# A two-column norm-weight tile is allocated behind the work buffers of the second sweep

## The chip, the core and the metric

The kernel runs on one core of a Trainium2 chip. A core has five engines that work side by side and wait for each other by semaphores: TensorE (PE, matrix products into PSUM), VectorE (DVE), ScalarE (ACT), GpSimd (POOL) and SyncE (SP, which here does nothing but issue DMA transfers, in its program's order). The metric is the device time of one execution in microseconds (us), the median of several runs. Changes under about 0.2% can't be told from none.

## The reference

One layer of an encoder over 2048 positions of width 1024, in float32. One input projection feeds two groups of heads. Group A is gated linear attention with a decay, summed over a forward and a backward scan in chunks. Group B is multi-head latent attention: low-rank q and kv with RMS norms, a shared rotary key, a full softmax. Both are gated, concatenated, projected once more, and added to the input under a layer norm:

```python
def hybrid_mixer(x, positions, w_in, ...):
    h = x @ w_in
    (g_q, g_k, g_v, g_gate, g_lr_f, g_lr_b, m_cq, m_ckv, m_kr, m_gate) = split(h)
    o_a = gla_branch(g_q, g_k, g_v, g_gate, g_lr_f, g_lr_b, ...)
    o_b = mla_branch(m_cq, m_ckv, m_kr, m_gate, positions, q_norm_g, w_uq, kv_norm_g, w_ukv)
    return concatenate([o_a, o_b]) @ w_out
x = layer_norm(alpha * x + hybrid_mixer(x, ...))
```

`mla_branch` normalises the compressed query with the weights `q_norm_g`, 256 numbers, before the product with `w_uq`. These 256 numbers are the tile that the change is about.

## The kernel before

Almost every product is made of three matmuls (`mm3`, lines 418 to 422): each float32 operand is split into a high part and a low remainder (`hi`, line 366, a copy on ACT; `lo`, line 372, a subtraction on DVE or POOL), and high times high (L420), one cross product (L421) and the other (L422) are summed in PSUM.

The work has four stages in time. The *first sweep* (`sweep_a`) goes backwards over 16 chunks of 128 positions and makes group A's projections, the scans' local parts and the gates; it stores its results (`qd_s`, `oi_s`, `su_s`, `u_s`) in DRAM. Two gates that are left over, of chunks 15 and 14, are made at its end (`late_gates`): the products `ipg` from the operands `xbh`, `xbl` (the split input of the chunk) and `wgh`, `wgl`, 24 matmuls for each chunk. The *second sweep* (`sweep_c`) goes forwards in eight steps of two chunks. It makes group B's projections (`ipm`, lines 1250 and on), gate (`pz`), the compressed keys, the query products `pqr` and `pq`, and finishes group A: `Ob` (L1418, L1419) is the product of the stored q (`qdb`, split to `qhb`, `qlb`) with the state. The state is carried by POOL: L1387 decays it, L1390 adds the stored `SU` of a chunk, L1395 scales it into `SU`, and `SU` is split to the two halves of `MMb` (L366 on ACT, L372 on POOL). Then comes *attention*, with `pS` and `o` as its large products, and at last the *output projection* with layer norm.

Before the first step the second sweep sets up weights (`SETUP_C`). `su_lset` (line 1131) issues seven loads on SP, in this order: `gq` (the q norm weights as 128 partitions of two numbers), `gkv_b`, `wkr` twice (`wqr` and `wkT` lie in the two halves of one tile of that name), `wqT`, and two small columns. `absorb_w` (L1165) then multiplies `wqT` with `wkT` on PE into `pabs`; `su_wS` (L1152, L1154) scales `gq` and then `wqr` by it on ACT; `scale_w` (L1170, DVE) scales `pabs` by `gq` and `gkv_b`. The loads of the first `SU` come behind these on SP.

The order of the instructions on each engine in the second sweep is set by a table of places (`PLACE_C` and the tables for the first and last step): every part has a number, the parts are sorted by it, and each engine works through its own in that order. The scheduler adds the waits. One of its rules matters here: a tile may be written only after the last use of whatever lay on the same bytes before (`reuse_waits="tile"`), so an address decides what a load waits for.

The on-chip memory is filled from two sides. On the left lie the constants, the input buffers, then for the second sweep the pools `wz`, `wm`, `bc` (weights and the split input `xch`, `xcl`), `wl` (loaded group A data: `ub`, `oib`, `qdb`, `SU`), `wk2` (work tiles; in the code `w1`) and `smc` (small tiles of norm sums; in the code `sm`). On the right lie, among others, the tiles of the late gates (`xab` with `xbh` and `xbl`, `wgp` with the gate weights). A pool's tile takes a multiple of 32 bytes in each partition.

Of the kernel before, what the change touches and what calls it, by code (L numbers as in the profile page):

```python
# [9 lines left out]
F32 = mybir.dt.float32  # L10
# [8 lines left out]
P = 128  # L19
# [336 lines left out]
class K:  # L356
# [773 lines left out]

    def su_lset(self):
        nc, ins, w1 = self.nc, self.ins, self.w1
        self.gq = self.bc.tile([P, 2], F32, name="gq")
        self.gkv_b = w1.tile([P, H, P], F32, tag="oT", name="gkv_b")[:, 0]
        t1 = w1.tile([P, 2, 512], F32, tag="qa", name="wkr")
        self.wkT = t1[:, 0].rearrange("p (h l) -> p h l", h=H)
        self.wqr = t1[:, 1].rearrange("p (c d) -> p c d", c=2)
        self.wqT = w1.tile([P, H, 256], F32, tag="gm", name="wqT")
        for t, n in ((self.gq, "gq_col"), (self.gkv_b, "gkv_bc"), (self.wqr, "wqr"), (self.wkT, "wkT"),
                     (self.wqT, "wqT"), (self.gkv_c, "gkv_col"), (self.gn_c, "gn_col")):  # L1140
            nc.sync.dma_start(t, ins[n])
        self.wa = [None, None]
# [869 lines left out]
```

## Time and profile before

| | |
|---|---|
| median of 3 runs | 1317.59 us |
| lowest and highest run | 1316.13 and 1318.52 us |
| profiled execution, first to last instruction (span) | 1311.9 us |
| mean granted clock of TensorE in it | 0.998 |
| PE busy | 1288.3 us, 98% of the span |
| DVE, ACT, POOL busy | 73%, 62%, 60% |
| first sweep and late gates | 0 to some 373 us of the span |
| second sweep | some 373 to 620 us |
| attention | some 620 to 1180 us |

The profiled execution is known by its span alone; the runs are timed from outside and include what lies around it. In the rows below, PE, DVE, ACT and POOL are the engines, SPq is the issuing of a DMA on SP's queue, L and a number is the line of the kernel. A row of the order of time has the start in us of the span, the duration in us, the engine, the line, the operation, the tile written and the tiles read, and in brackets the idle time of the engine just before it and who ended it. A row of a group has, after the bar, the busy time in us and the mean duration in ns. Matmuls are pipelined, so rows of PE overlap.

### The profile page before, as it was taken

What the parts mean: (1) busy time and instruction counts of PE and PEld (TensorE: products, weight loads), DVE (VectorE), ACT (ScalarE), POOL (GpSimd) and SP (SyncE); (2) the same over time, 40 slices, a digit from 0 to 9 for tenths busy, and PEclk for the clock granted to TensorE, in tenths of its full rate; (3) what the DMA queues carried; (4) which work ended last, traced back from release to release, by engine and by line L of the source; (5) the groups of instructions that cost most, each with busy time, mean ns of one, the idle gap of its engine ahead of it and who ended that gap; (6) DMA issues with size and microseconds to landing.
All of it is one profiled execution on the core that took longest, in us unless ns stands there. A gap on an engine that the chain in (4) does not pass through costs nothing.

```text
span 1311.9 us, 19981 instructions
## 1 busy us (share of the span) xinstructions
PE 1288.3 (98%) x7081; PEld 1129.9 (86%) x7081; DVE 958.5 (73%) x1712; ACT 812.5 (62%) x1339; POOL 784.6 (60%) x494
## 2 busy tenths in 40 slices
PE   7999999999999999999999999999999999999997
PEld 7999999999989999999788888888888887888786
DVE  7967684655675455554888888888888888468998
ACT  6765656555575656564687787888888888511110
POOL 0143333232457666671388888889999999844441
PEclk9999999999999999999999999999999999999999
DMA  8131313122475555565301111112223210366663
GB/s 283 61 100 53 93 53 92 49 76 71 147 245 173 197 194 177 201 202 177 121 1 41 41 42 41 41 57 59 63 66 102 51 41 9 121 208 174 210 195 121
DMA packets 107819, 145.81 MB, mean 111 GB/s; under 512 B 17250, under 2 KB 62694, under 8 KB 107720
## 3 DMA queue, kind: packets, MB, share of 16 engines
q1 hardware_dynamic: 99128, 142.41, 35.0%
q0 software_dynamic: 672, 2.10, 0.4%
q8 instruction: 56, 0.92, 0.3%
q10 hardware_dynamic: 7920, 0.03, 0.3%
q14 instruction: 43, 0.35, 0.2%
HBM read 94.14 MB, written 50.36 MB: 110 GB/s over the span
## 4 chain that ended last, share of the span: by engine, by line
PE 83%; DVE 4%; DMA 3%; ACT 2%; issue 2%; POOL 1%; SPq 1%; DVEq 0%; POOLq 0%; ACTq 0%
PE o L420 4%; PE o L421 4%; PE pS L1521 4%; PE pS L1524 4%; PE o L422 4%; PE pS L1523 4%; PE pS L1525 4%; PE pS L1522 4%; PE ipa L420 4%; PE ipa L422 4%; PE ipa L421 4%; PE pz L421 2%; PE pz L420 2%; PE pz L422 2%; PE ipg L420 2%; PE ipg L421 2%
## 5 line engine op out<-in xcount | busy, mean ns | idle before, releaser
L372 POOL TENSOR_TENSOR pl<-s,ph 128x1024 fp32r<-128x1024 f32 x128 | 306.9, 2412 | 66.7 <-ACT ph L366 61.5
L1543 DVE TENSOR_TENSOR rm<-pS,rm 128x512 f32<-128x512 f32 x210 | 144.8, 690 | 44.1 <-ACT s L1530 39.0
L1530 ACT ACTIVATE s<-pS 128x1024 f32<-128x1024 f32 x128 | 131.2, 1025 | 67.6 <-PE pS L1525 65.6
L1567 DVE TENSOR_TENSOR s<-s,mb 128x1024 f32<-128x1024 f32 x128 | 151.2, 1213 | 9.5 <-PE mb L1561 9.3
L1030 POOL TENSOR_TENSOR Us<-Us,cw 128x512 f32<-128x512 f32 x16 | 18.5, 1157 | 227.0 <-DVE Us L1028 175.2
L366 ACT ACTIVATE ph<-s 128x1024 fp32r<-128x1024 f32 x128 | 135.0, 1057 | 18.1 <-PE o L422 17.6
L1571 ACT ACTIVATE s<-s 128x1024 f32<-128x1024 f32 x128 | 131.4, 1050 | 13.8 <-DVE s L1567 13.7
L420 PE MATMUL ipa<-wah,xah 128*128 128x384 f32 (+1 forms) x384 | 130.6, 340 | 6.8 <-ACT wah L366 6.8
L422 PE MATMUL ipa<-wah,xal 128*128 128x384 f32 (+1 forms) x384 | 125.2, 326 | 0.0
L421 PE MATMUL ipa<-wal,xah 128*128 128x384 f32 (+1 forms) x384 | 125.0, 325 | 0.0
L1521 PE MATMUL pS<-qh,ckvT_h 128*128 128x512 f32 x256 | 103.7, 405 | 0.7 <-ACT s L1571 0.4
L420 PE MATMUL o<-ph,vh 128*128 128x512 f32 x256 | 102.6, 401 | 0.0
L422 PE MATMUL o<-ph,vl 128*128 128x512 f32 x256 | 101.3, 396 | 0.0
L1524 PE MATMUL pS<-rh,krs 128*128 128x512 f32 x256 | 101.2, 395 | 0.0
L421 PE MATMUL o<-pl,vh 128*128 128x512 f32 x256 | 101.1, 395 | 0.0
L1523 PE MATMUL pS<-qh,ckvT_l 128*128 128x512 f32 x256 | 100.9, 394 | 0.0
L1525 PE MATMUL pS<-rl,krs 128*128 128x512 f32 x256 | 100.7, 393 | 0.0
L1522 PE MATMUL pS<-ql,ckvT_h 128*128 128x512 f32 x256 | 100.6, 393 | 0.0
L1594 DVE TENSOR_TENSOR ap<-ap,s 128x512 f32<-128x512 f32 x120 | 83.1, 693 | 2.7 <-ACT s L1571 0.8
L372 POOL TENSOR_TENSOR ol<-of,oh 128x512 fp32r<-128x512 f32 x32 | 43.0, 1346 | 65.6 <-ACT oh L366 65.6
L420 PEld LDWEIGHTS ipa<-wah,xah 128*128 128x128 f32 x384 | 73.5, 192 | 7.6 <-ACT wah L366 6.8
L420 PE MATMUL pz<-xch,wzh 128*128 128x256 f32 x256 | 74.8, 292 | 0.0
(325 smaller groups left out, 3856.4 us busy)
## 6 DMA issues: line engine op xcount, KB each, us to landing
xcf<-xT_dram SPq DMA_DIRECT2D x16, 512.0 KB, 4.7
xr<-x_dram SPq DMA_DIRECT2D x16, 512.0 KB, 6.5
out_dram<-rr SPq DMA_DIRECT2D x32, 256.0 KB, 2.0
xaf<-xT_dram SPq DMA_DIRECT2D x14, 512.0 KB, 4.2
oib<-oi_s SPq DMA_DIRECT2D x16, 256.0 KB, 4.1
qdb<-qd_s SPq DMA_DIRECT2D x16, 256.0 KB, 4.6
SU<-su_s SPq DMA_DIRECT2D x16, 256.0 KB, 4.4
ub<-u_s SPq DMA_DIRECT2D x16, 256.0 KB, 4.7
```

Source lines behind the costliest of these rows:

```text
L366: return nc.scalar.activation(dst, src, AF.Copy).ins
L372: return e.tensor_tensor(dst, src, hi.bitcast(F32), ALU.subtract).ins
L420: mm(out, ah, bh, start=start, stop=False)
L421: mm(out, ah, bl, start=False, stop=False)
L422: mm(out, al, bh, start=False, stop=stop)
L1521: mm(ps[:, e], kh, qh, start=True, stop=False)
L1522: mm(ps[:, e], kh, ql, start=False, stop=False)
L1523: mm(ps[:, e], kl, qh, start=False, stop=False)
L1524: mm(ps[:, e], kr, rh, start=False, stop=False)
L1525: mm(ps[:, e], kr, rl, start=False, stop=True)
L1543: V.tensor_tensor(d["rm"], src[:, e], d["rm"], ALU.max)
L1567: V.tensor_tensor(s, s, d["mb"][:, None, :].to_broadcast([P, 2, QB]), ALU.subtract)
```

## The change

One line: the tile `gq` is taken from the pool `sm`, which is opened after the work buffers, in place of `bc`, which lies before them.

```diff
     def su_lset(self):
         nc, ins, w1 = self.nc, self.ins, self.w1
-        self.gq = self.bc.tile([P, 2], F32, name="gq")
+        self.gq = self.sm.tile([P, 2], F32, name="gq", bufs=1)
         self.gkv_b = w1.tile([P, H, P], F32, tag="oT", name="gkv_b")[:, 0]
```

In the built program this does the following. `gq` moves from byte 120000 of each partition to byte 178880. All tiles of `wl` and `wk2` move down by the 32 bytes that `gq` took in front of them, so their start addresses leave 192 modulo 256 where they left 224. The tiles of `sm`, and everything in attention, stay where they were. The instructions and their order on each engine are the same. Four waits differ: the load of `gq` waits for PE's count 2,255 (before 2,152), since its bytes now lie in `xbh` of chunk 14; the loads of `gkv_b` and `wqT` no longer wait for PE (before, counts 2,200 and 2,214); and the high split of the first output weight, `woh0`, on ACT waits for three DMA queues (before, four).

## The prediction

> **What bounds the kernel now.** I read the page first (shares, then the chain that ended last), then PE's waits in the second sweep, then, because the edit touches a load on SP's queue, the order of time of each engine around the start of that sweep.
>
> ```profile
> span 1311.9 us, 19981 instructions
> PE 1288.3 (98%) x7081; PEld 1129.9 (86%) x7081; DVE 958.5 (73%) x1712; ACT 812.5 (62%) x1339; POOL 784.6 (60%) x494
> PE 83%; DVE 4%; DMA 3%; ACT 2%; issue 2%; POOL 1%; SPq 1%; DVEq 0%; POOLq 0%; ACTq 0%
> ```
>
> TensorE is busy 98% of the span and holds 83% of the chain. So whatever stops PE is paid in full, and whatever any other engine does is free until it makes PE wait. PE's own waits from 375 to 460 us of the span (who was waited for, total, times, longest) are these:
>
> ```profile
> PE Ob L1419 <- POOL qlb L372: 0.8, 1, 0.8
> PE ipm L422 <- POOL xcl L372: 0.4, 1, 0.4
> PE Ob L1418 <- DVE gm L1209: 0.3, 1, 0.3
> ```
>
> There is next to nothing to win there, and the first row shows a place without slack: at the first Ob product of the sweep, PE already waits for POOL.
>
> **The change part by part.** No instruction is added, removed or reordered on any queue. Three things change: addresses of the work buffers, the place of the 8-byte tile gq, and the waits that follow from what lay at these places before.
>
> *The wait of gq's load.* The old place was last used by tiles of the first sweep; the new one lies inside xbh of chunk 14, the stationary operand of the last late gate. In the built program the load is therefore released at PE's 2,255th count in place of the 2,152nd: the last read of that xbh, the L421 matmul below. SP's queue as it stood:
>
> ```profile
> 365.26 0.38 SPq L1141 DMA_DIRECT2D gq<-gq_col_dram  x1
> 365.74 0.38 SPq L1141 DMA_DIRECT2D gkv_b<-gkv_bc_dram  x1
> 369.60 0.33 SPq L1141 DMA_DIRECT2D wkr<-wqr_dram  x1
> ...
> 370.50 1.22 SPq L1141 DMA_DIRECT2D wqT<-wqT_dram  x1
> ...
> 372.98 0.84 SPq L1369 DMA_DIRECT2D SU<-su_s  x2
> ```
>
> ```profile
> 372.89 0.39 PE L421 MATMUL ipg<-wgl,xbh 128*128 128x512 f32 x1
> ...
> 378.00 0.37 PE L422 MATMUL ipm<-wmh,xcl 128*128 128x448 f32 x1
> 378.21 1.95 PE L1165 MATMUL pabs<-wkr,wqT 128*128 128x128 f32 x16
> ```
>
> That matmul ends at 372.89 + 0.39 = 373.28, so gq is issued at 373.3 in place of 365.26. Everything behind it on SP waits too. The queue itself lost some of this time before, so not all 8 us count: gkv_b came 0.48 after gq, and then wkr stood until 369.60 for a store of the first sweep:
>
> ```profile
> SPq L1141 <- DMA su_s<-Us: 3.3, 1, 3.3
> ```
>
> By 373 that store is long down. So wkr goes out at 373.28 + 0.48 + 0.48 = 374.24, which is 4.6 later than 369.60, and the loads behind it keep their spacing: wqT at 375.1, SU at 377.6. The PE waits that gkv_b and wqT lose had been met before their issue, and cost nothing either way.
>
> Who waits for these loads? Two things on PE's path. First pabs, which reads wkr and wqT:
>
> ```profile
> wqT<-wqT_dram SPq DMA_DIRECT2D x1, 512.0 KB, 4.9
> ```
>
> It landed at 370.50 + 4.9 = 375.4, with 2.8 us of cover before pabs at 378.21. Landing at 380.0 it breaks that cover by 1.8 us. Second, POOL's chain that makes the operands of the first Ob product. It begins with SU:
>
> ```profile
> 378.48 1.66 POOL L1390 TENSOR_TENSOR Sf<-Sf,SU 64x512 f32<-64x512 f32 x1 [5.37 <-DMA SU<-su_s]
> 380.21 1.37 POOL L1395 TENSOR_TENSOR SU<-Sf,cw 64x512 f32<-64x512 f32 x1
> 381.66 1.03 POOL L1387 TENSOR_TENSOR Sf<-Sf,cw 64x512 f32<-64x512 f32 x1
> ...
> 384.30 1.29 POOL L372 TENSOR_TENSOR MMb<-SU,MMb 128x512 fp32r<-128x512 f32 x1
> 385.56 1.27 POOL L372 TENSOR_TENSOR qlb<-qdb,qhb 128x512 fp32r<-128x512 f32 x1
> ```
>
> ```profile
> 385.75 0.28 PE L1418 MATMUL Ob<-MMb,qhb 128*128 128x256 f32 x1
> 386.88 0.33 PE L1419 MATMUL Ob<-MMb,qlb 128*128 128x128 f32 x1 [0.85 <-POOL qlb L372]
> ```
>
> POOL sits idle 5.37 us until SU lands, then runs without a break to 386.83, and PE waits for that. If SU lands 4.6 later, POOL starts at 383.1. It then runs a little faster: the first two of its operations ran beside DVE's eight wzl splits, which will be over by then, and the same operations take less elsewhere (shortest, median, longest of three):
>
> ```profile
> 374.71 5.97 DVE L372 TENSOR_TENSOR wzl<-wzr,wzh 128x512 fp32r<-128x512 f32 x8
> L1390 POOL TENSOR_TENSOR Sf<-Sf,SU x3: 1274/1288/1659, 378.5 to 390.3; 64x512 f32<-64x512 f32 x3
> L1395 POOL TENSOR_TENSOR SU<-Sf,cw x3: 1033/1035/1370, 380.2 to 397.0; 64x512 f32<-64x512 f32 x3
> ```
>
> That returns 1.66 - 1.29 and 1.37 - 1.03, together 0.7 us. qlb ends 4.6 - 0.7 = 3.9 later, and Ob goes on at 390.8. The 1.8 us at pabs are inside these 3.9, not added: PE reaches Ob at 387.6, and waits there some 2.9 us (390.8 less 387.6 and the 0.28 of the first matmul) where it waited 0.85. ACT's share is no later: its MMb split (382.38 before) stands behind the second POOL operation, now done at 383.1 + 1.29 + 1.03 = 385.4, and MMb's low half on POOL comes after 388. Nothing takes the 3.9 back: the later waits of PE in the first table are on chains that PE itself starts (pz to gm, gm to xcl), so they move along.
>
> [...]
>
> *The addresses* (as the two built programs have them). The loads' buffers and the work buffers move 32 bytes down, from residue 224 to 192 modulo 256. In 288 matmuls of the sweep (192 of pq, 96 of pqr) one operand lay at 224 and the other at 192; now both lie at 192. In Ob both lay at 224 and both move; for the transposes ident stays at 128. What is a match worth? Mean durations (after the bar: busy us, mean ns):
>
> ```profile
> L422 PE MATMUL pq<-cqT_h,wabs_l 128*128 128x256 f32 x64 | 18.0, 281 | 0.0
> L420 PE MATMUL pq<-cqT_h,wabs_h 128*128 128x256 f32 x64 | 17.9, 280 | 0.0
> L421 PE MATMUL pq<-cqT_l,wabs_h 128*128 128x256 f32 x64 | 17.8, 278 | 0.0
> L422 PE MATMUL pz<-xch,wzl 128*128 128x256 f32 x256 | 72.3, 282 | 0.0
> L422 PE MATMUL o<-ph,vl 128*128 128x512 f32 x256 | 101.3, 396 | 0.0
> L422 PE MATMUL px<-woh,ol 128*128 128x512 f32 x56 | 21.8, 389 | 0.0
> ```
>
> pz has both operands at 192 and the width of pq, and is no faster: 282 against 278 to 281. At width 512, px (both at 192) beats o (0 and 192) by 7 ns. So the two ends are a loss of 192 x 2.3 ns = 0.4 us (282 less the mean of 280, 278, 281), and a gain of 288 x 7 ns = 2.0 us. I take the loss of 0.4, since those rows have the width and the very operands.
>
> *The split of woh0* on ACT loses one of four DMA waits, hundreds of us into attention. No row shows it as a wait of PE: 0.
>
> *Sum.* +3.9 + 0.4 = +4.3 us. The profiled execution is known by its span of 1311.9; the median of the runs, 1317.59, is 5.7 above it, and I leave that margin as it is: a span of 1316.2, a time of 1321.9.
>
> **The rivals.**
> (a) *Clock.* PE would stand for 1.8 us and soon after for 2.9. The end of the trace shows a drop (PE busy, weight loads, DVE, ACT, POOL, clock, DMA):
>
> ```profile
> 1304.20:1306.50 2.30, 0.00 (x0) 0.00 (x0) 2.20 (x6) 0.41 (x2) 0.00 (x0) 1.00 0.00 0
> 1306.50:1311.00 4.50, 0.00 (x0) 0.00 (x0) 2.28 (x7) 0.00 (x0) 0.00 (x0) 0.51 0.30 117
> ```
>
> After 2.3 us without a matmul the granted clock is half. A gap of 2.9 could do that. If PE then needs about as long, 3 to 4 us, to come back at half speed, this costs 1.5 to 2 more: 1323.4 to 1323.9. [...]
> (b) *The loads are quicker.* DMA has nothing queued just before 373, so SU could land sooner after its issue than before. Only pabs' 1.8 and less would be left: with 0.4, about 1319.8, and 1319.0 if SU is 2.5 us sooner and the residue counts nothing. Against it: the SU of before was issued behind the same loads.
> (c) *Faster.* The match gives more than any row shows: it decides from 3.9 us upward, 13.5 ns of each of 288 matmuls, twice what px has over o. To be seen as faster it needs 3.9 + 2.6 = 6.5 us, 22.6 ns each, and then the time is 1315.0 or less. Against it: pz above.
> (d) *It does nothing*: both waits have cover that I overlooked, and the residue is worth 0: 1317.6. For it speaks only that SP was early at gq by 8 us before.
>
> **How the numbers follow.** Forecast 0.60; (a) 0.12; (b) 0.17; (d) 0.07; (c) 0.04. Predicted: 1321.9. Range 1319.0 to 1324.0: it takes in (b) and (a), and the gain of 2.0 (1319.5), and leaves out (c) and (d). A change under 0.2%, 2.6 us, can't be told from none here. Slower by more, above 1320.2: forecast and (a), with a little less for the gain of 2.0, 0.73; within: (b), (d) and that part, 0.23; faster 0.04.
>
> **What would show it.** Right: gq issued at 373.3 and SU at 377.6; PE waiting some 1.8 before pabs and some 2.9 at the first Ob for POOL's qlb; POOL's first Sf near 1.29; pq near 282; the rest of the span the same length. Wrong: SU landing less than 4 us later, a clock below 1.00 between 380 and 400, pq clearly under 278, or new waits of PE after 400.

## The result: 4.3 us slower

| | before | after |
|---|---|---|
| median of 11 runs each, same chip | 1316.13 us | 1320.37 us |
| lowest to highest run | 1314.53 to 1318.52 us | 1317.56 to 1325.36 us |
| ratio after to before | | 1.0033, 95% interval 1.0024 to 1.0043 |
| profiled execution's own time | | 1322.9 us |
| its span, first to last instruction | 1311.9 us | 1320.8 us |
| mean granted clock of TensorE in it | 0.998 | 0.996 |

The ratio is a loss of 4.3 us, with an interval of 3.2 to 5.7 us. The prediction was +4.3 and 1321.9 us; the time is 1.5 us lower than that because the kernel before has a median of 1316.13 us over all its 11 runs, 1.5 us below that of its first three.

The first two lines of the profile page of the changed kernel show a PE that has hardly more to do than before: 1292.1 against 1288.3 us, part of it (below) at a lower clock. The loss is time in which it stands or runs slowly.

```profile
span 1320.8 us, 19978 instructions
PE 1292.1 (98%) x7081; PEld 1133.1 (86%) x7081; DVE 957.7 (73%) x1712; ACT 813.2 (62%) x1339; POOL 783.7 (59%) x494
```

SP's queue at the start of the second sweep, in order of time (start, duration, line, tile):

```profile
372.81 0.33 SPq L1141 DMA_DIRECT2D gq<-gq_col_dram  x1
373.19 0.42 SPq L1141 DMA_DIRECT2D gkv_b<-gkv_bc_dram  x1
373.78 0.33 SPq L1141 DMA_DIRECT2D wkr<-wqr_dram  x1
...
374.63 0.43 SPq L1141 DMA_DIRECT2D wqT<-wqT_dram  x1
...
376.12 0.84 SPq L1369 DMA_DIRECT2D SU<-su_s  x2
```

`gq` now goes out at 372.81 instead of 365.26, and everything behind it follows at once: `wqT` 4.1 us later than before, `SU` 3.1 us later. PE and POOL in the same stretch:

```profile
377.50 0.37 PE L422 MATMUL ipm<-wmh,xcl 128*128 128x448 f32 x1
380.61 2.95 PE L1165 MATMUL pabs<-wkr,wqT 128*128 128x128 f32 x16 [2.74 <-DMA wqT<-wqT_dram]
...
389.81 0.28 PE L1418 MATMUL Ob<-MMb,qhb 128*128 128x256 f32 x1
...
390.23 0.33 PE L1419 MATMUL Ob<-MMb,qlb 128*128 128x128 f32 x1
```

```profile
382.55 1.26 POOL L1390 TENSOR_TENSOR Sf<-Sf,SU 64x512 f32<-64x512 f32 x1 [9.96 <-DMA SU<-su_s]
383.89 1.03 POOL L1395 TENSOR_TENSOR SU<-Sf,cw 64x512 f32<-64x512 f32 x1
...
388.89 1.29 POOL L372 TENSOR_TENSOR qlb<-qdb,qhb 128x512 fp32r<-128x512 f32 x1
```

Compare the start of the same matmul in both traces. The last `ipm` product ahead of `pabs` is 0.50 us earlier than before (377.50 against 378.00), a difference carried in from the start of the execution. The first L1419 of `Ob` is 3.35 later (390.23 against 386.88). Between these two the changed kernel loses 3.85 us. That is the main loss, in one place 13 us long.

PE's waits from 375 to 460 us (who was waited for: total, times, longest) say where PE stood:

```profile
PE pabs L1165 <- DMA wqT<-wqT_dram: 2.7, 1, 2.7
PE ipm L422 <- POOL xcl L372: 0.4, 1, 0.4
PE Ob L1418 <- DVE gm L1209: 0.3, 1, 0.3
```

The wait for `qlb` at the first `Ob` is gone, and a longer one for `wqT` stands at `pabs`. The rest of the 3.85 is in the clock. In the table by stretch (stretch and its length; busy us of PE, weight loads, DVE, ACT, POOL, with the number of instructions; granted clock; DMA share; GB/s):

```profile
375.50:380.60 5.10, 2.37 (x12) 1.88 (x11) 3.89 (x7) 3.81 (x8) 0.00 (x0) 1.00 0.66 204
380.60:384.90 4.30, 4.29 (x24) 4.30 (x25) 1.55 (x5) 1.35 (x3) 2.27 (x2) 0.60 0.89 343
384.90:389.80 4.90, 4.90 (x42) 4.90 (x42) 1.61 (x7) 3.69 (x12) 4.74 (x6) 1.00 0.67 216
```

The clock at its lowest is 0.50 (from 382 to 384 us), so a mean of 0.60 over 4.30 us is 3.4 us at half clock ((1.00 - 0.60) / 0.5 x 4.30). `pabs` then takes 2.95 us instead of 1.95. PE comes to `Ob` just as POOL finishes `qlb` (388.89 + 1.29 = 390.18), so it no longer waits there.

The span is 8.9 us longer, not 4.3. The other large part lies in the output projection, which the change does not touch:

```profile
1223.84 0.47 PE L420 MATMUL pmb<-woh,oh 128*128 128x512 f32 x1 [3.63 <-DVE rr L1927]
```

```profile
1224.50:1228.00 3.50, 3.50 (x10) 2.72 (x9) 3.40 (x7) 0.93 (x3) 0.77 (x1) 0.51 0.83 260
```

A load of `x` landed late there (DVE waited 9.4 us for it), PE stood 3.6 us where it stood 0.9 before, and the clock fell once more. In a second profile of the changed kernel this wait is 1.2 us and the clock does not fall there (0.997 over that whole execution, 0.996 over this one), and in the other traces of this case it is 0.9 to 2.1 us. So it is an event of one execution, and nothing shows that the change brings it.

### The profile page after: what moved, and what is told of

Same layout as the page of the kernel before. It is cut to its first block, busy times and chain, and to the rows that moved or that the text cites. A ratio compares the mean times of both kernels' runs of the same rounds, so it can differ in the third digit from the quotient of the medians.

```text
span 1320.8 us, 19978 instructions
## 1 busy us (share of the span) xinstructions
PE 1292.1 (98%) x7081; PEld 1133.1 (86%) x7081; DVE 957.7 (73%) x1712; ACT 813.2 (62%) x1339; POOL 783.7 (59%) x494
## 4 chain that ended last, share of the span: by engine, by line
PE 83%; DVE 4%; ACT 3%; DMA 2%; POOL 2%; issue 2%; SPq 0%; DVEq 0%; POOLq 0%; ACTq 0%
PE o L420 4%; PE o L421 4%; PE o L422 4%; PE pS L1521 4%; PE pS L1524 4%; PE pS L1523 4%; PE pS L1525 4%; PE pS L1522 4%; PE ipa L420 4%; PE ipa L422 4%; PE ipa L421 4%; PE pz L421 2%; PE pz L422 2%; PE pz L420 2%; PE ipg L420 2%; PE ipg L421 2%
```

## The experiments

The theory after the result: the late wait of `gq` holds up SP's queue; two chains hang on it, `wqT` to `pabs` on PE and `SU` to `qlb` on POOL; the later of the two decides, and the dropped clock after the wait at `pabs` costs nothing as long as POOL ends last. The rivals: the addresses of the matmul operands carry the loss, or the dropped clock does.

**The wait alone.** The kernel before, with `gq` in its new place and an unused tile of the same size in the old, so that all work buffers stay at 224 modulo 256:

```diff
-        self.gq = self.bc.tile([P, 2], F32, name="gq")
+        self.bc.tile([P, 2], F32, name="pad")
+        self.gq = self.sm.tile([P, 2], F32, name="gq", bufs=1)
```

> The tile at its new place, but the 32 bytes it left are held by an unused tile, so the work buffers stay at residue 224. Theory (the wait of gq's load on SP's queue is the loss): SP goes on at about 373, SU is late by 3 to 4 us, the first Ob product by 3.9, pq stays at 278 to 281 ns: kernel before + 3.9 us (+3 to +5). Rival (the addresses of the work buffers are the loss): no change, within 1 us of the kernel before. Rival (chance alone, dropped clocks): the spans differ by dropped clocks and the first Ob product comes no later.

Measured: 1319.0 us against 1314.75 for the kernel before on the same chip; ratio 1.0032, interval 1.002 to 1.0044. SP, PE and POOL do as in the changed kernel (SP's queue in order of time, PE's wait, and POOL in order of time):

```profile
373.06 0.33 SPq L1142 DMA_DIRECT2D gq<-gq_col_dram  x1
```

```profile
PE pabs L1166 <- DMA wqT<-wqT_dram: 2.6, 1, 2.6
```

```profile
382.06 1.25 POOL L1391 TENSOR_TENSOR Sf<-Sf,SU 64x512 f32<-64x512 f32 x1 [9.18 <-DMA SU<-su_s]
```

The whole loss is there without any change of a work buffer's address. One thing differs from the changed kernel: POOL got `SU` earlier, and had just finished `qlb` (388.40 + 1.29 = 389.69) when PE came to `Ob`:

```profile
388.40 1.29 POOL L372 TENSOR_TENSOR qlb<-qdb,qhb 128x512 fp32r<-128x512 f32 x1
```

```profile
389.91 0.28 PE L1419 MATMUL Ob<-MMb,qhb 128*128 128x256 f32 x1
```

Here PE itself ended last, by 0.2 us, through its wait at `pabs` and the dropped clock behind it (a mean of 0.86 from 380 to 392 us; `pabs` took 2.94 us). The two chains end so close together that either of them can be the later one.

**The addresses alone.** The changed kernel, with the load of `gq` taken out of `su_lset` and issued behind the first loads of `SU`:

```diff
-SETUP_C = ("lset", "u15", "u14", "wS", "wH", "wL", "pb0", "wa0", "wh0", "wl0", "pb1", "wa1", "wh1", "wl1")
+SETUP_C = ("lset", "gq", "u15", "u14", "wS", "wH", "wL", "pb0", "wa0", "wh0", "wl0", "pb1", "wa1", "wh1", "wl1")
...
+    gq=-1.0,
...
-        for t, n in ((self.gq, "gq_col"), (self.gkv_b, "gkv_bc"), (self.wqr, "wqr"), (self.wkT, "wkT"),
+        for t, n in ((self.gkv_b, "gkv_bc"), (self.wqr, "wqr"), (self.wkT, "wkT"),
...
+    def su_gq(self):
+        self.nc.sync.dma_start(self.gq, self.ins["gq_col"])
```

> The changed kernel with gq's load issued behind the first two SU loads in place of ahead of the set-up loads: the work buffers are at residue 192, and gq's wait holds nothing up. Theory (the wait): no late SU, no wait of PE at pabs; what is left is the dearer pq (283 in place of 280 ns on the mean, 192 of them: 0.6 us): kernel before + 0.4 to + 1.0 us. Rival (the addresses): still some 4 us over the kernel before.

Measured: 1315.21 us against 1314.75; ratio 1.0002, interval 0.9993 to 1.001. SP's queue, PE's wait and one group of `pq` (busy us, mean ns after the bar):

```profile
370.40 0.33 SPq L1142 DMA_DIRECT2D wkr<-wqr_dram  x1
...
372.83 2.30 SPq L1373 DMA_DIRECT2D SU<-su_s  x2
375.23 0.38 SPq L1146 DMA_DIRECT2D gq<-gq_col_dram  x1
```

```profile
PE Ob L1423 <- POOL qlb L373: 0.8, 1, 0.8
```

```profile
L423 PE MATMUL pq<-cqT_h,wabs_l 128*128 128x256 f32 x64 | 18.1, 283 | 0.0
```

With the buffers at 192 and the queue free, PE waits as in the kernel before and no loss can be measured. `pq` is at 283 ns all the same, so the address does set it; it is only worth little.

**Where the wait is taken.** The changed kernel with the `pabs` products placed later on PE, so that they cannot wait for `wqT`:

```diff
-    pb0=-0.328,
+    pb0=-0.012,
...
-    pb1=-0.256,
-    wa1=-0.068,
+    pb1=-0.011,
+    wa1=-0.01,
```

> The changed kernel with pabs put behind the first four pz parts, so that PE has work while wqT lands. Theory (POOL's chain from SU sets the end, the wait at pabs lies inside it): no wait at pabs, but PE then waits some 4 us at the first Ob product, which goes on at about 390 as in the changed kernel: kernel before + 3.9 to + 4.5; a clock dropped in that gap would no longer be hidden, and adds up to 1.7: at most + 6. Rival (the 2.7 us wait at pabs is itself the loss): it goes away, and the kernel is at before + 1 to + 2.

Measured: 1320.97 us; ratio 1.0046, interval 1.0032 to 1.006, that is 6.0 us. The wait moved to `Ob` and, with both waits there, came to 3.2 us:

```profile
388.40 0.58 PE L1418 MATMUL Ob<-MMb,qhb 128*128 128x256 f32 x1 [2.58 <-POOL MMb L372]
...
389.63 0.48 PE L1419 MATMUL Ob<-MMb,qlb 128*128 128x128 f32 x1 [0.65 <-POOL qlb L372]
```

So POOL's chain alone holds PE for 3.2 us. Counted from the last `ipm` product ahead of `pabs`, the first L1419 is 2.8 us later than in the kernel before, less than the 3.9 of the changed kernel, since POOL had `SU` sooner in this execution (382.00). After it the matmuls themselves are slow (0.58 and 0.48 us, where the changed kernel has 0.28 and 0.33): here the clock fell at that wait, for 3.8 us at half speed up to 392 (a mean of 0.84 over 12 us from 380), and `pz` still takes 0.41 us in place of 0.28 until 394.8. That is some 6.6 us in all, about twice as long as in the changed kernel. Nothing hides that any more: by the first `Ob` of the next chunk the 2.8 us have become 5.3.

**Without the dropped clock.** The changed kernel with 14 idle matmuls ahead of `pabs`, so that PE hardly stands there (their results are overwritten):

```diff
+        if ct == 0:
+            for _ in range(14):
+                self.nc.tensor.matmul(pa.rearrange("p h l -> p (h l)")[:, :448], self.xch[:, 0, 0], self.Wm[0][0],
+                                      start=True, stop=True)
```

> The changed kernel with 14 idle matmuls of 448 columns (2.8 us, their result is overwritten) ahead of pabs, so that PE does not stand still while wqT lands. Theory (the dropped clock in the changed kernel's profile is hidden by POOL's chain): no drop near 381, pabs at full speed, PE waits instead for qlb at the first Ob product, 1 to 2 us; same time as the changed kernel within 1 us, before + 3.5 to + 4.5. Rival (the dropped clock costs 1.5 us or more of the 4.3): faster than the changed kernel by that much, before + 2 to + 3.

Measured: 1319.32 us; ratio 1.0036, interval 1.0024 to 1.0048. The mean granted clock is 0.999, and there is no drop in this stretch (1.00 from 380 to 392 us):

```profile
377.56 3.00 PE L1166 MATMUL pabs<-wmh,xch 128*128 128x448 f32 x14
...
381.65 2.02 PE L1169 MATMUL pabs<-wkr,wqT 128*128 128x128 f32 x16 [1.09 <-DMA wqT<-wqT_dram]
...
390.68 0.33 PE L1423 MATMUL Ob<-MMb,qlb 128*128 128x128 f32 x1 [0.84 <-POOL qlb L372]
```

`pabs` takes 2.02 us again, PE reaches `Ob` earlier, waits 0.84 us for `qlb`, and no gain can be measured. The comparison is not clean, since the loads landed later in this execution (`wqT` 7.0 us after its issue, where the changed kernel took 5.8) and POOL's chain with them, by 0.6 us. The changed kernel's own rows say it more directly: without the drop PE, with the 7.54 us from `pabs` to `Ob` of the kernel before in place of 9.20, would have come to `Ob` 1.7 us earlier, at 388.1, and would have waited until `qlb` was done at 390.18. In that execution the dropped clock was hidden under POOL's chain.

**State loads first, in both kernels.** The two `SU` loads placed ahead of the set-up loads, once in the kernel before and once in the changed one:

```diff
-    lS=(-1.12, -1.093),
+    lS=(-1.32, -1.31),
```

> The kernel before with the loads of the first two SU put ahead of the set-up loads on SP's queue. Theory (the first Ob product is set by SU's landing): SU goes out at 370 to 371 in place of 373.0, POOL's chain ends 2 to 3 us earlier, PE's wait of 0.85 for qlb goes away, and wqT, 1 us later, still lands ahead of pabs: kernel before - 0.8 us (-0.3 to -1.0). Rival (the wait at Ob has another cause, or wqT becomes the bound): no change, or up to 1 us slower.

> The changed kernel with the loads of the first two SU put ahead of gq, so that only the set-up loads stand behind gq's wait. Theory (two covers are broken, and POOL's chain is the later one): PE no longer waits for qlb at Ob, but still some 2 to 3 us for wqT at pabs; then that wait sets the time, + 2.2 at pabs + 0.6 for pq - 0.85 at Ob = + 2.0, and a clock dropped in the gap is no longer hidden, + 1.4: kernel before + 2.0 to + 3.4. Rival (SU alone matters): kernel before + 0.6 or less. Rival (neither order matters): before + 4.3.

Measured: the kernel before becomes slower, 1318.61 us against 1314.98, ratio 1.0032 (1.002 to 1.0044). The changed kernel hardly gains, 1317.97 us, ratio 1.0025 (1.0014 to 1.0037), that is +3.3 us. In the kernel before with this edit, SP's queue and PE:

```profile
369.90 1.88 SPq L1141 DMA_DIRECT2D gq<-gq_col_dram  x1
...
372.60 0.37 SPq L1141 DMA_DIRECT2D wkr<-wqr_dram  x1
...
373.54 0.39 SPq L1141 DMA_DIRECT2D wqT<-wqT_dram  x1
```

```profile
379.86 2.57 PE L1165 MATMUL pabs<-wkr,wqT 128*128 128x128 f32 x16 [1.92 <-DMA wqT<-wqT_dram]
```

The first was a miss. I had not counted that the issue of `gq`, which moves 1 KB, would take 1.88 us behind two `SU` loads (0.38 before). The loads of `gq` and `gkv_b`, which used to go out while the queue waited for the store, now stand behind that wait too. All this puts `wqT` 3.0 us later than before and breaks the other cover. Nor did POOL gain by the early `SU`. It had it at 373.12, but its four operations on the state then took 1.81, 1.37, 1.37 and 1.59 us, where the changed kernel has 1.26, 1.03, 1.03 and 1.29. I take it that they ran beside DVE's eight `wzl` splits, as the first two do in the kernel before (there the splits took 5.97 us, in the changed kernel, with none beside them, 5.07). DVE's `rope`, which comes behind the splits and was done at 381.93 in the kernel before, was late, and POOL stood for it:

```profile
384.85 0.33 POOL L1295 TENSOR_TENSOR krf<-krf,rope 128x64 f32<-128x64 f32 x1 [5.36 <-DVE rope L1470]
```

So `qlb` was done at 388.47, against 386.83 in the kernel before. The changed kernel with this edit has the same wait of 5.36 us, and PE's other wait by itself:

```profile
381.90 2.95 PE L1165 MATMUL pabs<-wkr,wqT 128*128 128x128 f32 x16 [3.35 <-DMA wqT<-wqT_dram]
```

PE now stands 3.35 us at `pabs`, and not at `Ob`; the loss stays at some 3 us. The clock falls here too (a mean of 0.86 from 380 to 392 us), and this time it is paid: PE takes 9.19 us from `pabs` to `Ob` where it took 7.54 before, and comes there at 391.09, when `qlb` has been done for 2.0 us. Taking `SU` off `gq`'s wait leaves `wqT` behind it.

**Other residues.** The kernel before with an unused tile in front of the work buffers, which puts them at 0 and at 64 modulo 256 (one run each; the diff is that for 0, and `[P, 24]` gives 64):

```diff
+        self.bc.tile([P, 8], F32, name="pad")
```

> The kernel before with 32 unused bytes more ahead of the work buffers: residue 0 in place of 224, waits of gq's load as before. If a common residue is what makes pq dearer, pq stays near 280 ns here as in the kernel before; if each residue has its own price, anything from 278 to 290. The product Ob, both operands at one residue again, stays at 331 ns. Time: kernel before within 1 us.

> The same with 96 unused bytes: residue 64, so that the operands of pq lie 128 bytes apart modulo 256. pq near 280 ns if only a common residue is dear. Time: kernel before within 1 us.

Measured: 1314.17 and 1314.61 us against 1314.98. The three groups of `pq` take 280, 279 and 280 ns at residue 0 and 282, 281 and 281 at 64; one row of the kernel at residue 0:

```profile
L420 PE MATMUL pq<-cqT_h,wabs_h 128*128 128x256 f32 x64 | 17.9, 280 | 0.0
```

Of four residues, the one that matches the other operand (192 with 192, 283 ns) is the slowest, by 1 to 5 ns. A single run each can't say more on the whole time than that nothing large hangs on it.

**An attempt to gain.** The kernel before with only `wkT` and `wqT` loaded first, then `SU`, then the other five set-up loads:

```diff
...
+    lset2=-1.0,
...
-        for t, n in ((self.gq, "gq_col"), (self.gkv_b, "gkv_bc"), (self.wqr, "wqr"), (self.wkT, "wkT"),
-                     (self.wqT, "wqT"), (self.gkv_c, "gkv_col"), (self.gn_c, "gn_col")):
+        for t, n in ((self.wkT, "wkT"), (self.wqT, "wqT")):
...
+    def su_lset2(self):
+        for t, n in ((self.gq, "gq_col"), (self.gkv_b, "gkv_bc"), (self.wqr, "wqr"), (self.gkv_c, "gkv_col"),
+                     (self.gn_c, "gn_col")):
...
```

> The kernel before with its set-up loads in the order in which PE and POOL need them: wkT and wqT, then the first two SU, then gq, gkv_b, wqr and the two small columns. Theory (PE's wait of 0.85 at the first Ob product is set by the landing of SU, and pabs by that of wqT): both land earlier, the wait goes away, PE does not stand still at pabs: kernel before - 0.4 to - 0.9 us, which the times can hardly tell from none, but the rows can. Rival (a load that now stands later becomes late: wqr or gq on ACT ahead of the MMb split): no gain or up to 2 us slower.

Measured: a miss, 1315.86 us against 1313.9; ratio 1.0018 (1.001 to 1.0027), 2.4 us slower. POOL in order of time, then PE's waits:

```profile
375.60 1.54 POOL L1395 TENSOR_TENSOR Sf<-Sf,SU 64x512 f32<-64x512 f32 x1 [3.09 <-DMA SU<-su_s]
377.21 1.37 POOL L1400 TENSOR_TENSOR SU<-Sf,cw 64x512 f32<-64x512 f32 x1
...
384.18 0.32 POOL L1300 TENSOR_TENSOR krf<-krf,rope 128x64 f32<-128x64 f32 x1 [2.45 <-DVE rope L1475]
385.26 1.29 POOL L373 TENSOR_TENSOR MMb<-SU,MMb 128x512 fp32r<-128x512 f32 x1 [0.76 <-ACT MMb L367]
```

```profile
PE Ob L1424 <- POOL qlb L373: 0.8, 1, 0.8
PE pz L423 <- DVE wzl L373: 0.6, 2, 0.4
```

`SU` landed 2.9 us earlier than in the kernel before (375.60 against 378.48), but POOL gave it back: its four early operations had the longer durations again (1.54, 1.37, 1.37 and 1.62 us), then it stood 2.45 us for `rope` and 0.76 us for ACT. It is the course seen with the state loads first: PE was still waiting for a `wzl` split just before 383.12, where all eight were done by 380.68 in the kernel before, and what DVE and ACT do behind them was late, `pz` too (0.6 us). In this trace the first `Ob` product with `qlb` is 1.6 us later than in the kernel before and attention 1.8; what is left of the 2.4 us was not settled. No version tried is shown to be faster than the kernel before.

**The changed kernel again**, for a second profile:

> The changed kernel once more, beside the kernel before on the same chip. Theory: kernel before + 3.9 to + 4.5; the first Ob product goes on some 3.9 us later again and pq is at 283 ns; the second dropped clock of the first profile, in the output projection, was chance and need not come back, and without it the span is some 4 to 5 us over 1311.9. Rival (the second drop belongs to the change): it is there again, at the same place, some 4 us dear.

Measured: 1318.23 us against 1313.9; ratio 1.0032 (1.002 to 1.0044), span 1316.7. PE in order of time:

```profile
379.60 2.02 PE L1165 MATMUL pabs<-wkr,wqT 128*128 128x128 f32 x16 [2.10 <-DMA wqT<-wqT_dram]
...
388.27 0.38 PE L1418 MATMUL Ob<-MMb,qhb 128*128 128x256 f32 x1 [0.90 <-POOL MMb L372]
389.49 0.48 PE L1419 MATMUL Ob<-MMb,qlb 128*128 128x128 f32 x1 [0.84 <-POOL qlb L372]
```

In this execution the wait at `pabs` was 2.10 us and left the clock alone, and PE waited 1.74 us more at `Ob`: nearly the split that the prediction had drawn. The clock fell behind that second wait, where nothing hides it: the mean from 380 to 392 us is 0.89, which is 2.6 us at half speed, and `ipm` still takes 0.57 us in place of 0.37 until 392.65, so it is some 3.4 us again. Counted as above, the first L1419 is 3.5 us late and the first `Ob` of the next chunk 5.0; in the first profile both are 3.9 late. In attention the two executions are 5.4 and 5.2 us late. The same kernel has two courses here, with nearly the same sum.

## Why the prediction was right

**The wait of `gq`'s load: right.** Forecast 373.3; 372.81, or 373.3 with the 0.50 us by which this whole trace runs early. That `wkr` and the loads behind it follow at once, with no further wait, was right as well.

**`SU` 4.6 us later: mis-sized at SP, right at POOL.** `SU` went out only 3.1 us later, or 3.6 without the 0.50, because the issue of `wqT` took 0.43 us instead of 1.22 and that of the last small column 0.43 instead of 0.64; the prediction had kept the old spacing. But POOL got it at 382.55, forecast 383.1: with the same 0.50 that is equal. What was gained in the issue was lost behind it: from the issue of `SU` to POOL's start 6.4 us passed, where it was 5.5. `wqT` shows the same (transfer, size, us from issue to landing), 5.8 us where it took 4.9:

```profile
wqT<-wqT_dram SPq DMA_DIRECT2D x1, 512.0 KB, 5.8
```

That gain and loss cancelled is luck. In the other traces with the same queue, reckoned in the same way, POOL started between 1.0 us before the forecast (the later `pabs`) and 0.5 after it (the filled gap).

**POOL takes 0.7 back: right.** 1.26 and 1.03 us for the two operations that had taken 1.66 and 1.37, now that DVE's `wzl` splits are over (at 379.27).

**Ob 3.9 later, the wait at `pabs` inside it: right in the sum, wrong in its parts.** The two traces give 3.85 us, and the second profile of the changed kernel 3.5. The forecast of 1.8 us at `pabs` was 2.74 in one profile and 2.10 in the other, and that of 2.9 at `Ob` was next to nothing and 1.74. The step that failed is the landing of `wqT`, taken at 4.9 us after its issue, which was 5.8 and 5.2. The parts do not matter while POOL's chain ends last, as the prediction had it, and that held in both profiles of the changed kernel. But it has little room: with the wait alone PE ended last by 0.2 us, and with the state loads first in the changed kernel by 2.0.

**The clock, rival (a): it happened, and was paid in one of two executions.** A clock under 1.00 between 380 and 400 stood in the prediction as a sign against it, and it is there. It came at the other wait, at `pabs`, after 2.74 us. PE from the start of `pabs` to the first `Ob` took 9.20 us (380.61 to 389.81) against 7.54 before (378.21 to 385.75), so a drop costs PE 1.7 us, in the 1.5 to 2 that was forecast. But in that execution PE had that much time to spare. A drop is paid where PE ends last: behind the wait at `Ob`, as rival (a) had it, and at `pabs` when POOL is done first (state loads first, in the changed kernel). The later `pabs` shows the first of these, 6.0 us instead of 4.3, though the intervals of the two overlap, and so does the second profile of the changed kernel, from 3.5 to 5.0 us. So the sum, which put the clock at nothing, describes one of the two profiled executions and rival (a) the other; how often each comes is not known. The 0.12 for (a) was an estimate. The clock fell after 1.92 us (state loads first, in the kernel before) and 2.74 us here, and not after 2.10 us in the second profile. The 3 to 4 us at half speed were an estimate too, for no row of before shows PE at work at a lowered clock; in the changed kernel a drop lasted 3.4 us, with the later `pabs` some 6.6.

**The addresses: the right sign, slightly more.** The groups of `pq` after:

```profile
L422 PE MATMUL pq<-cqT_h,wabs_l 128*128 128x256 f32 x64 | 18.1, 283 | 0.0
L421 PE MATMUL pq<-cqT_l,wabs_h 128*128 128x256 f32 x64 | 18.1, 283 | 0.0
L420 PE MATMUL pq<-cqT_h,wabs_h 128*128 128x256 f32 x64 | 18.1, 283 | 0.0
```

283 against a mean of 279.7 is 192 x 3.3 ns = 0.64 us, where 0.4 was forecast from `pz`. The gain of 2.0 us (and with it rival (c)) is out: a match of the two operands' residues gains nothing at this width. By the time alone this cannot be told from nothing (address alone: -0.9 to +1.3 us).

**No new wait after `Ob`: right, but for small ones.** From `Ob` to attention the two traces drift apart by another 1.3 us in the first profile of the changed kernel and, once the drop is over, by 0.4 in the second. `pq` can explain the 0.4; the rest is in part a wait for `xcl` of 0.3 us that the second profile does not have, and in part open. One trace can drift by that much without a cause in the change: the one at residue 64, which has none of the late loads, is 0.7 us later at attention than that of the kernel before.

Rivals (b) and (d) fell with the same rows: neither wait had a cover that was overlooked, and `SU` landed as late as the sum had it, or up to 1.0 us sooner in other traces, not the 2.5 of (b).

**The sum: right, and closer than its parts.** The medians differ by 4.2 us, with an interval of 3.2 to 5.7, and the two profiled executions of the changed kernel are 5.2 and 5.4 us late in attention. An agreement with 4.3 to a tenth is therefore luck. What is shown is the wait, the two chains behind it, and a loss of 3.2 to 5.7 us.

## What to carry to other kernels

An address on the chip can be a wait. Before moving a tile, ask what lay on its new bytes last, on which engine's count its first write will then wait, and which queue that write stands in: here a load of 1 KB, needed much later, held two large loads behind it. Price such a delay at the end of each chain that hangs on the queue, take the later and not the sum, and count as hidden whatever an engine loses while that chain is still running. Where two chains end within some tenths of a microsecond of each other, price both, for either can be the later one. And before a load is moved forward, ask what its consumer will then run beside: POOL, started early, took 1.81 us for an operation of 1.26 and then stood 5.36 us for DVE's `rope`.

## What the runs showed that was not expected

- The clock fell after gaps of different lengths: after 1.92 us (state loads first, in the kernel before), 2.74 (the changed kernel) and 3.35 (state loads first, in the changed kernel) at `pabs`, and in the second profile of the changed kernel after two of 0.90 and 0.84 us close together at `Ob`; it did not after 2.10 us at `pabs` in that same profile, nor after 1.09 us in the filled gap. So in these runs the length of the gap alone did not decide.
- The fall can come after PE has gone on. In the changed kernel the gap ended at 380.61, and the mean clock is still 0.87 from 380 to 382 us and 0.50 from 382 to 384, so half speed began near 381.5.
- POOL and DVE took longer side by side here. DVE's eight `wzl` splits took 5.07 us in the changed kernel, with no operation of POOL beside them, and 5.97 in the kernel before with two; these two took 1.66 and 1.37 us there, and 1.26 and 1.03 in the changed kernel.
- The issue of a load took its queue very different times. `gq` took 1.88 us right behind two `SU` loads (state loads first, in the kernel before) and 0.33 when 2.8 us lay between them (the same in the changed kernel). With the addresses alone and with the products first it took 0.38 and 0.42 right behind them, but there the two `SU` loads took 2.30 and 2.02, against 0.81. The order of loads on one queue can therefore move more than the bytes of each would suggest.
- Loading the state first made the kernel before slower by as much as the change did. Its order of loads sits between two chains, of which one has 2.8 us of cover (`wqT`) and the other none (`SU`), and the earlier `SU` did not help POOL: it had it 5.4 us sooner (373.12 against 378.48) and was done with `qlb` 1.6 us later (388.47 against 386.83).
